# Splits of out-projection weights held behind softmax maxima, one FFN split moved back by one place, and the scaling of a head's output moved to the next head's second step

## The chip, the cores and the metric

The kernel runs on one core of a Trainium2 chip. The metric is the device time of one launch in microseconds (us). TensorE is PE in the profile (PEld is its weight load), VectorE is DVE, ScalarE is ACT, GpSimd is POOL, and SyncE, which only issues DMAs here, is SP. Every engine runs its own instructions strictly in the order in which they stand, and waits on semaphores for the others.

## The reference, cut to what matters

One transformer block on 512 tokens of width 1024 in fp32 (shapes after the batch and layer axes are dropped):

```python
h = rms_norm(x, attn_norm_g);  z = h @ w_in                    # 512 x 1952
y_mla  = softmax(q k^T * 96**-0.5 + mask) v                    # 8 heads, q and k 96 wide, v 64 wide
y_diff = rms_norm((softmax(q0 k0^T/8 + bias + mask)            # 4 heads, two maps of 64, v 128 wide
                 - lam * softmax(q1 k1^T/8 + bias + mask)) v, out_g) * (1 - lam_init)
x += concat[y_mla, y_diff] @ w_out                             # 1024 x 1024
g = rms_norm(x, ffn_norm_g) @ w_gate                           # 2816 wide
x += (silu(causal_dwconv3(g)) * (rms_norm(x, ffn_norm_g) @ w_up)) @ w_down
x += sigmoid(rms_norm(x, ple_norm_g) @ w_ple_gate) * (p @ w_ple_proj)
```

## The kernel before, in words

**Precision by splitting.** TensorE multiplies in a shortened fp32 format (fp32r). Each fp32 operand is therefore split into a rounded high part and a low remainder, and each product is made of three matmuls: high x high (L155), high x low (L156) and low x high (L157, in the helper `mm3`). `load_w` (L140 to L150) does this for a weight: one DMA on SP's queue brings 128x1024 floats (512 KB) into a buffer `raw` (L140), ACT casts it to `hi` (L148), DVE subtracts to get `lo` (L149). During attention there are three `raw` buffers, used in turn, so a DMA waits until the subtraction of the weight three places before it has read its buffer. The same pair of ACT cast and DVE subtraction makes the activations' halves: `split` (L183, L184; with a gain per channel L186, L187).

**Stages.** (1) From 0 to about 70 us, the norm and the projections. (2) From about 70 to 161 us, the loop over 32 slots (8 MLA heads x 4 blocks of 128 queries). Each slot makes the logits `ml` of the slot after it (PE), their negated maximum `nm` (DVE L570, L571), exp (ACT L573, tile `pm`), transposes `pm` on PE (L538, `pTm`), copies the result (`pt`; in odd steps ACT L541, in even steps DVE L543), and multiplies by V (PE L583, `mo`). Between these steps the projections for the second attention (`zd`) and later the first out-projection units are pumped as filling. (3) From about 161 to 224 us, the loop over 16 slots of the differential attention (`dslots`, 4 heads x 4 steps), which runs two slots ahead with the logits: PE makes two maps `dl`, one DVE instruction adds the bias strip and reduces to the maximum (L675, tiles `pmd`, `nmd`), ACT takes exp (L676), DVE joins both maps (L680 to L682), PE transposes (`pTd`), ACT copies (L541), PE multiplies by V (`do`). When a head's fourth step is through, `diff_pv` has ACT square and copy the output (`sqo`, `yd`, L696, L697), DVE reduce it (L699, L703), POOL take the power -1/2 (L704, `ro`), and DVE scale `yd` by `ro` (L706). Two steps into the next head `y_split` transposes it for the out-projection. The queries and keys of the next head come from `diff_T` (PE transposes `d0T` and `d1T`, split into the `st` tiles). Filling here is the out-projection (`wo_units`, tile `o`; DVE adds each finished block to `x`, L631). Its eight weights are `o00` to `o03` for the MLA half and `o10` to `o13` for the other half. (4) From about 224 to 250 us, the rest of the out-projection and the FFN's norm. (5) From about 250 to 600 us, the FFN: weights `wA`, `wT`, `wS` are split on ACT (L824) and DVE (L828), PE makes `g`, `gx`, `u` and so on from them, DVE does the convolution `cv` (L1112), and the down-projection `dn` follows. (6) The gate at the end.

**What sets the order.** PE's order is that of the program throughout (a manual schedule). For DVE and ACT a scheduler chooses the order in stage 2 (from its fifth slot on), 3 and 4; `tc.issue_after(ins)` tells it to place an instruction no earlier than behind `ins`. In the prologue and in the FFN's ramp (from L848 to the `region.__exit__` some 50 us into the FFN) DVE, ACT and POOL stand as written too. SP's DMAs stand in program order. In the loop before, the weights of `o` are loaded by `wo_w` when `wo_units` first asks for them, with nothing that holds their splits back; the scheduler has put the splits where its estimate found room, from 115 us on.

Of the kernel before, what the change touches and what calls it, by code (L numbers as in the profile page):

```python
# [15 lines left out]
ALU = mybir.AluOpType  # L16
# [4 lines left out]
P = 128  # L21
T = 512
NT = 4
# [4 lines left out]
H = 8  # L28
QK = 96
DH = 4  # L30
# [59 lines left out]
def _f32(ap):  # L90
    return ap.bitcast(F32)
# [3 lines left out]
def hybrid_block(ctx: ExitStack, tc: tile.TileContext, a: dict, out: bass.AP):  # L95
    nc = tc.nc
    V, S, G, TE = nc.vector, nc.scalar, nc.gpsimd, nc.tensor
# [11 lines left out]
    def bank(tag, name):  # L109
        return pp_.tile([P, 512], F32, tag=tag, bufs={"acc": 2, "lg": 3, "tp": 2, "ob": 1}[tag], name=name)  # L110

    def tt(name, dtype=F32):
        return att.tile([P, T], dtype, tag="tt", bufs=16, name=name)

    def sq_tile(name):
        return att.tile([P, D], F32, tag="sq", bufs=2, name=name)

    def pm_tile(name):
        return att.tile([P, T], F32, tag="pm", bufs=PM, name=name)
# [10 lines left out]
    def th_tile(name):  # L130
        return wts.tile([P, T], F32R, tag="th", bufs=8, name=name), wts.tile([P, T], F32R, tag="tl", bufs=8, name=name + "l")
# [6 lines left out]
    def load_raw(src, n, name):  # L138
        raw = wp["rawpool"].tile([P, 1024], F32, tag="raw", bufs=wp["raw"], name=f"raw_{name}")
        nc.sync.dma_start(raw[:, :n], src)  # L140
        return raw

    def load_w(src, n, name, eng=None):

        raw = load_raw(src, n, name)
        hi = wp["pool"].tile([P, 1024], F32R, tag="hi", bufs=wp["w"], name=f"hi_{name}")
        lo = wp["pool"].tile([P, 1024], F32R, tag="lo", bufs=wp["w"], name=f"lo_{name}")
        S.copy(hi[:, :n], raw[:, :n])  # L148
        (eng or V).tensor_tensor(lo[:, :n], raw[:, :n], _f32(hi[:, :n]), op=ALU.subtract)  # L149
        return hi, lo  # L150
# [153 lines left out]
    def d_hi(kq):  # L304
        raw = load_raw(a["w_d"][0, kq], 1024, f"d0{kq}")
        w = [wts.tile([P, 1024], F32R, tag=i, bufs=NW, name=f"{i}_d0{kq}") for i in ("hi", "lo")]
        zw.append(w)
        return (*hi(raw, w[0]), w[1])

    zw, zw1, zw2, wuq, wukv = [], [], [], [[], []], []  # L310
    d0 = d_hi(0)
# [168 lines left out]
    for t in range(NT):  # L480
        kv_ = kvb[:, t]
        sqk = sq_tile("sqk")[:, :H * 64].rearrange("p (h d) -> p h d", d=64)
        for c in range(2):
            hs = slice(4 * c, 4 * c + 4)
            ps = bank(UP_BANKS[(2 * t + c) % 4], f"ukv{t}{c}")
# [18 lines left out]
    for t in range(NT):  # L504
        q_ = xn_tile(f"qn{t}")[:, :H * QK].rearrange("p (h d) -> p h d", d=QK)
        sq = sq_tile("sqq")[:, :H * QK].rearrange("p (h d) -> p h d", d=QK)
        for c in range(2):
            hs = slice(4 * c, 4 * c + 4)
            ps = bank(UP_BANKS[(2 * t + c) % 4], f"uq{t}{c}")
# [50 lines left out]
    mla, ymn = {}, []  # L560
# [30 lines left out]
    strips = []  # L591
# [21 lines left out]
    def y_split(i, src, col, tag):  # L613

        ps = bank(tag, f"yT{i}")
        for t in range(NT):
            TE.transpose(ps[:, tsl[t]], src[:, tsl[t]], ident)
        yh[i], yl[i] = th_tile(f"yh{i}")
        split(yh[i], yl[i], ps, col)
# [10 lines left out]
    def add_x(b, ps):  # L630
        V.tensor_tensor(xb(b), xb(b), ps, op=ALU.add)  # L631

    wo2 = {}

    def wo_w(kq, dq):
        return load_w(a["w_out"][kq, dq], 1024, f"o{kq}{dq}")

    def wo_units(kq, dqs, nk):
# [13 lines left out]
    df = {}  # L652

    def diff_T(h, c):
        ps = bank("tp" if h else "acc", f"d{c}T{h}")
        for t in range(NT):
            TE.transpose(ps[:, tsl[t]], zd[c][t][:, h * P:(h + 1) * P], ident)
        h_, l_ = st[4 * (h % 2) + 2 * c], st[4 * (h % 2) + 2 * c + 1]
        split(h_, l_, ps, dcol if c == 0 else None)
        df["qk", h, c] = (h_, l_)  # L660

    def diff_logits(h, t):
        n = (t + 1) * P
        if t == 0:
            df["s0", h] = sm.tile([P, NT], F32, tag="s0", name="s0")
        s0 = df["s0", h][:, t:t + 1]
        (qh_, ql_), (kh_, kl_) = df["qk", h, 0], df["qk", h, 1]
        pms, s1 = [], sm.tile([P, 1], F32, tag="s1", bufs=4, name="s1")
        for m in range(2):
            r = slice(64 * m, 64 * m + 64)  # L670
            ps = bank("lg", f"dl{h}{t}{m}")
            mm3(ps[:, :n], [(qh_[r, tsl[t]], ql_[r, tsl[t]], kh_[r, :n], kl_[r, :n])])
            pm = pm_tile("pmd")
            nm = sm.tile([P, 1], F32, tag="nm", bufs=4, name="nmd")
            V.tensor_tensor_reduce(out=pm[:, :n], in0=ps[:, :n], in1=strips[0][:, h, T - n:], scale=1.0, scalar=3e38, op0=ALU.add, op1=ALU.min, accum_out=nm)  # L675
            S.activation(pm[:, :n], pm[:, :n], AF.Exp, bias=nm, scale=-1.0, accum_out=s0 if m == 0 else s1)  # L676
            pms.append(pm)

        cf = sm.tile([P, 1], F32, tag="cf", bufs=4, name="cf")
        V.reciprocal(cf, s1)  # L680
        V.scalar_tensor_tensor(cf, cf, nlam, s0, op0=ALU.mult, op1=ALU.mult)
        V.scalar_tensor_tensor(pms[0][:, :n], pms[1][:, :n], cf, pms[0][:, :n], op0=ALU.mult, op1=ALU.add)  # L682
        df["pm", h, t] = pms[0]

    def diff_pv(h, t):
        if t == 0:
            df["po"] = bank("ob", f"do{h}")
        po, pt = df["po"], df.pop(("pt", h, t))
        for j in range(t + 1):
            TE.matmul(po[:, tsl[t]], pt[:, tsl[j]], zd[2][j][:, h * P:(h + 1) * P], start=j == 0, stop=j == t)  # L690
        if t < NT - 1:
            return
        s0 = df["s0", h]
        yn = tt(f"yd{h}")
        sq = sq_tile("sqo")[:, :T]
        S.activation(sq, po, AF.Square)  # L696
        df["copy"] = S.copy(yn, po)  # L697
        sso = sm.tile([P, NT], F32, tag="sso", name="sso")
        V.reduce_sum(sso, sq.rearrange("p (t d) -> p t d", d=P), axis=AX.X)  # L699

        mo, ro = sm.tile([P, NT], F32, tag="mo", name="mo"), sm.tile([P, NT], F32, tag="ro", name="ro")
        V.scalar_tensor_tensor(mo, s0, EPS, s0, op0=ALU.mult, op1=ALU.mult)
        V.scalar_tensor_tensor(mo, sso, 1.0 / P, mo, op0=ALU.mult, op1=ALU.add)  # L703
        G.tensor_tensor(ro, mo, mhalf[:, :NT], op=ALU.pow)  # L704
        yv = yn.rearrange("p (t d) -> p t d", d=P)
        df["scale"] = V.tensor_tensor(yv, yv, ro.unsqueeze(2).broadcast_to([P, NT, P]), op=ALU.mult)  # L706
        df["y", h] = yn

    dslots = [(h, t) for h in range(DH) for t in range(NT)]
    x_sb = []  # L710
# [19 lines left out]
    for i, (h, t) in enumerate(slots):  # L730
        if i < 2:
            (mla_q, mla_k)[t](1)
        if i + 1 < len(slots):
            mla_logits(*slots[i + 1])
        if i == 4:
            region.__exit__(None, None, None)
            held = tc.issue_after(mla["nm"].ins)
            held.__enter__()
        if i == 8:
            held.__exit__(None, None, None)  # L740
            with tc.issue_after(mla["k"].ins):
                zd_norm(0)
        if 0 < h < H - 1 and t < 2:
            (mla_q, mla_k)[t](h + 1)
        if i == 1:
            lo(*z1_hi(3))
        if i in (9, 11, 13, 15):
            with tc.issue_after(mla["nm"].ins):
                zw2.append(load_w(a["w_d"][2, len(zw2)], 1024, f"d2{len(zw2)}"))
        if h < H - 1:  # L750
            pump(FILL_MLA[t])
        if i == 6:
            bias_strip()
        if h == H - 1:
            if t == 0:
                pump(100)
                fill.append(wo_units(0, range(4), 4))
            last_mla[t]()
        mla["pt", h, t] = probs_T(mla.pop(("pm", h, t)), t, f"m{h}{t}", t % 2)
        if i:  # L760
            mla_pv(*slots[i - 1])
# [3 lines left out]
    diff_T(1, 1)  # L765
    pump()
    y_split(3, ymn[3], None, "tp")
    for i, (h, t) in enumerate(dslots):
        if i + 2 < len(dslots):
            diff_logits(*dslots[i + 2])  # L770
        pump(FILL_DIFF[h][t])
        df["pt", h, t] = probs_T(df.pop(("pm", h, t)), t, f"d{h}{t}", True)
        if i:
            diff_pv(*dslots[i - 1])
        if h + 1 < DH and t == 0:
            diff_T(h + 1, 0)
        if t == 3 and h + 2 < DH:
            diff_T(h + 2, 1)
        if h and t == 2:
            y_split(4 + h - 1, df["y", h - 1], ocol, "tp")  # L780
        if h and t == 3:
            if h == 2:
                fill.append(wo_units(1, range(2), 2))
# [19 lines left out]
    for b in order[:6]:  # L803
        n = len(early)
# [22 lines left out]
    def lo_(h_, l_, src):  # L827
        V.tensor_tensor(l_, src, _f32(h_), op=ALU.subtract)  # L828
        return h_, l_
# [61 lines left out]
    for b in order:  # L891
        if b in early:
            ps = early[b]
            mm3(ps, wo_blocks(7, 8, b, wo2[b // 2]), False, True)
        else:
            ps = bank("tp" if b == 3 else "lg", f"o3{b}")
# [314 lines left out]
    d0 = down_hi(0)  # L1211
# [1 line left out]
    next(new)  # L1213
    next(g)
    up_split(2, cv2)
    dn0 = [lo_(*d0)]
    w5 = w_steps(5)
    old, g = g, new
    next(g)
    next(w5)  # L1220
    next(w4)
    next(old)
    w6 = w_steps(6)
# [6 lines left out]
    d0 = down_hi(1)  # L1230
# [80 lines left out]
    for b in (6, 7):  # L1311
        ps = bank("lg", f"dn4{b}")
# [27 lines left out]
    ps = [pg_bank(b) for b in range(4)]  # L1340
# [100 lines left out]
```

## Time and profile before

| | |
|---|---|
| median of 3 runs | 653.76 us (653.20, 653.76, 653.77) |
| the profiled execution | 653.42 us, its span in the profile 651.6 us |
| TensorE's granted clock | 1.000 |
| weights of `o`, first DMA issued, last cast begun | 103.4 us, 198.0 us |

The span begins with the first instruction in the trace and ends with the last; the other 1.8 us of the profiled execution lie outside it. All times in the trace count from the span's start. A row of the timeline gives start, duration, engine, line, operation, output, input, shapes, and in square brackets how long the engine had been idle before it and what it waited for. A row that was put together from x4 equal instructions has the time from the first one's start to the last one's end. On DVE and ACT an instruction begins 0.07 to 0.11 us before the one ahead of it ends, so a 1.22 us subtraction holds the next one back by 1.13 us.

### The profile page before, as it was taken

How to read it: one execution, taken by the hardware profiler on the slowest of the kernel's cores; microseconds unless marked ns; L12 is line 12 of the kernel's file. 1: busy time of each engine (PE TensorE's matmuls, PEld its weight loads, DVE VectorE, ACT ScalarE, POOL GpSimd, SP SyncE). 2: the span in 40 equal slices, each digit the busy share in tenths (PEclk: the TensorE clock that was granted, in tenths of full speed). 3: DMA queues.
4: the chain of work that ended last, by engine and by line, in shares of the span. 5: the costliest groups of instructions: out<-in, count | busy, mean ns of one | idle time of the engine just before them, and what ended most of it. 6: DMA issues, size and time to landing. Idle time of an engine off the chain costs nothing.

```text
span 651.6 us, 10276 instructions
## 1 busy us (share of the span) xinstructions
PE 641.6 (98%) x3932; PEld 569.5 (87%) x3932; DVE 475.2 (73%) x860; ACT 362.9 (56%) x631; POOL 56.6 (9%) x93
## 2 busy tenths in 40 slices
PE   9999999999999999999999999999999999999997
PEld 9988888888777778889999999999999999988886
DVE  6789587656878677888886767677767676759444
ACT  7797666457666455556554555455454545637211
POOL 1520040000000121000100000000010000000000
PEclk9999999999999999999999999999999999999999
DMA  8241235234100248636675646565646453531121
GB/s 303 96 162 40 91 73 171 66 115 144 33 33 2 64 179 254 162 70 178 174 215 127 179 114 181 122 197 116 179 114 177 116 176 114 179 130 60 38 80 49
DMA packets 29912, 82.63 MB, mean 127 GB/s; under 512 B 3100, under 2 KB 4124, under 8 KB 29736
## 3 DMA queue, kind: packets, MB, share of 16 engines
q1 hardware_dynamic: 23816, 69.17, 31.9%
q0 software_dynamic: 5616, 12.33, 11.1%
q8 instruction: 31, 0.51, 0.3%
q10 hardware_dynamic: 432, 0.49, 0.2%
q14 instruction: 17, 0.14, 0.1%
HBM read 77.77 MB, written 5.52 MB: 128 GB/s over the span
## 4 chain that ended last, share of the span: by engine, by line
PE 88%; DVE 7%; ACT 3%; issue 1%; DMA 1%; POOL 0%; ACTq 0%; DVEq 0%; POOLq 0%
PE dn L157 6%; PE dn L156 6%; PE dn L155 6%; PE gx L157 4%; PE gx L155 4%; PE gx L156 4%; PE g L155 4%; PE g L156 4%; PE g L157 4%; PE zd L155 3%; PE zd L157 3%; PE zd L156 3%; PE pg L155 2%; PE pg L157 2%; PE pg L156 2%; PE u L155 2%
## 5 line engine op out<-in xcount | busy, mean ns | idle before, releaser
L828 DVE TENSOR_TENSOR wSl<-rS,wSh 128x1024 fp32r<-128x1024 f32 x21 | 25.7, 1224 | 44.5 <-ACT wSh L824 44.4
L157 PE MATMUL dn<-ah,lo_dn 128*128 128x512 f32 x144 | 56.4, 392 | 0.0
L156 PE MATMUL dn<-al,hi_dn 128*128 128x512 f32 x144 | 56.3, 391 | 0.0
L155 PE MATMUL dn<-ah,hi_dn 128*128 128x512 f32 x144 | 56.0, 389 | 0.0
L945 POOL DMA_DIRECT2D rS<-in_w_gu x19 | 22.7, 1195 | 250.9 <-DVE cv L1112 115.0
L824 ACT CAST wSh<-rS 128x1024 fp32r<-128x1024 f32 x21 | 22.1, 1051 | 35.8 <-PE gy L156 35.5
L155 PE MATMUL zd<-hi_d,xh 128*128 128x512 f32 x96 | 39.4, 410 | 0.0
L156 PE MATMUL zd<-lo_d,xh 128*128 128x512 f32 x96 | 37.5, 391 | 0.0
L631 DVE TENSOR_TENSOR x<-x,dn 128x512 f32<-128x512 f32 x44 | 29.8, 678 | 6.5 <-PE dn L157 6.3
L828 DVE TENSOR_TENSOR wTl<-rA,wTh 128x1024 fp32r<-128x1024 f32 x19 | 23.3, 1224 | 14.9 <-ACT wTh L824 14.3
L573 ACT ACTIVATE pm<-ml,nm,rq 128x128 f32<-128x128 f32 (+3 forms) x32 | 19.7, 617 | 22.7 <-DVE nm L571 22.7
L157 PEld LDWEIGHTS dn<-ah,lo_dn 128*128 128x128 f32 x144 | 27.0, 187 | 5.7
L155 PEld LDWEIGHTS dn<-ah,hi_dn 128*128 128x128 f32 x144 | 27.1, 188 | 5.2
L156 PEld LDWEIGHTS dn<-al,hi_dn 128*128 128x128 f32 x144 | 27.0, 188 | 5.3
L155 PE MATMUL o<-yh,hi_o 128*128 128x512 f32 x64 | 26.9, 420 | 1.0 <-DVE x L631 1.0
L1115 ACT ACTIVATE cv<-cv 128x512 f32<-128x512 f32 x22 | 13.9, 631 | 24.5 <-DVE cv L1112 24.4
L824 ACT CAST wAh<-rA 128x1024 fp32r<-128x1024 f32 x21 | 22.0, 1050 | 9.1 <-DMA rA<-in_w_gu 9.1
L570 DVE TENSOR_REDUCE nm<-ml 128x1 f32<-128x128 f32 (+3 forms) x32 | 15.6, 486 | 15.3 <-PE ml L157 15.3
L155 PE MATMUL g<-b2h,wAh 128*128 128x256 f32 (+1 forms) x88 | 26.3, 299 | 0.1
L676 ACT ACTIVATE pmd<-pmd,nmd 128x128 f32<-128x128 f32 (+3 forms) x32 | 17.9, 560 | 15.1 <-DVE nmd L675 15.1
L156 PE MATMUL g<-b2l,wAh 128*128 128x256 f32 (+1 forms) x88 | 26.2, 297 | 0.0
L157 PE MATMUL g<-b2h,wAl 128*128 128x256 f32 (+1 forms) x88 | 26.2, 297 | 0.0
(467 smaller groups left out, 2226.8 us busy)
## 6 DMA issues: line engine op xcount, KB each, us to landing
rA<-in_w_gu SPq DMA_DIRECT2D x22, 512.0 KB, 3.9
rS<-in_w_gu SPq DMA_DIRECT2D x22, 512.0 KB, 3.5
rS<-in_w_gu POOLq DMA_DIRECT2D x19, 512.0 KB, 6.0
raw_dn<-in_w_down SPq DMA_DIRECT2D x18, 512.0 KB, 5.9
raw_d<-in_w_d SPq DMA_DIRECT2D x12, 512.0 KB, 3.7
r<-in_w_gu SPq DMA_DIRECT2D x19, 256.0 KB, 6.5
raw_o<-in_w_out SPq DMA_DIRECT2D x8, 512.0 KB, 3.7
rS_pg<-in_w_pg SPq DMA_DIRECT2D x6, 512.0 KB, 3.9
```

Of the source, the lines that this page charges most:

```text
L155: TE.matmul(ps, xh, wh, start=first and i == 0, stop=False, skip_group_check=again)
L156: TE.matmul(ps, xh, wl, start=False, stop=False, skip_group_check=again)
L157: TE.matmul(ps, xl, wh, start=False, stop=last and i == n - 1, skip_group_check=again)
L570: V.reduce_max(nm, ps[:, :n], axis=AX.X, negate=True)
L573: S.activation(pm[:, :n], ps[:, :n], AF.Exp, bias=nm, scale=r, accum_out=mla["ssum", h // 2][:, t, h % 2:h % 2 + 1])
L631: V.tensor_tensor(xb(b), xb(b), ps, op=ALU.add)
L676: S.activation(pm[:, :n], pm[:, :n], AF.Exp, bias=nm, scale=-1.0, accum_out=s0 if m == 0 else s1)
L824: S.copy(h_, src)
L828: V.tensor_tensor(l_, src, _f32(h_), op=ALU.subtract)
L945: nc.gpsimd.dma_start(sums[f].rearrange("p (i c) -> p i c", i=2), a["w_gu"][f][:, :2048].rearrange("p (i c) -> p i c", i=2)[:, :, :512], a ...
L1115: S.activation(cv, cv, AF.Silu)
```

## The change

Three edits, all in the order of the work; no arithmetic is changed.

1. The weights of `o` get a dictionary `wo_first`. Weight `o00` is now asked for in the third step of the last MLA head, and the scheduler is told to place its cast and its subtraction no earlier than behind the maximum of the last MLA slot (`mla["nm"]`). `o01`, `o02`, `o03`, `o10` and `o11` are asked for in the differential loop in slots 0, 3, 7, 10 and 12, each behind the maximum that was issued last (`df["nm"]`, which is that of two slots later). `wo_units` takes them from the dictionary. `o12` and `o13` are asked for after the loop as before.
2. `diff_pv` no longer issues the scaling `yd*ro` at once. It stores it, and the loop issues it in the second step of the next head. The last head is scaled at once, as before.
3. In the FFN's ramp the subtraction of the first down-projection weight (`lo_dn`) moves behind two generator steps, the second of which is that of `wAl` of unit 5.

```diff
+        if (kq, dq) in wo_first:
+            return wo_first.pop((kq, dq))
         return load_w(a["w_out"][kq, dq], 1024, f"o{kq}{dq}")
...
-            V.tensor_tensor_reduce(out=pm[:, :n], in0=ps[:, :n], in1=strips[0][:, h, T - n:], scale=1.0, scalar=3e38, op0=ALU.add, op1=ALU.min, accum_out=nm)
+            df["nm"] = V.tensor_tensor_reduce(out=pm[:, :n], in0=ps[:, :n], in1=strips[0][:, h, T - n:], scale=1.0, scalar=3e38, op0=ALU.add, op1=ALU.min, accum_out=nm)
...
-        df["scale"] = V.tensor_tensor(yv, yv, ro.unsqueeze(2).broadcast_to([P, NT, P]), op=ALU.mult)
         df["y", h] = yn
+        df["scaling"] = lambda: V.tensor_tensor(yv, yv, ro.unsqueeze(2).broadcast_to([P, NT, P]), op=ALU.mult)
+        if h == DH - 1:
+            df["scale"] = df["scaling"]()
...
+        if h == H - 1 and t == 2:
+            with tc.issue_after(mla["nm"].ins):
+                wo_first[0, 0] = wo_w(0, 0)
...
+    PRE = {0: (0, 1), 3: (0, 2), 7: (0, 3), 10: (1, 0), 12: (1, 1)}
...
+        if i in PRE:
+            with tc.issue_after(df["nm"].ins):
+                wo_first[PRE[i]] = wo_w(*PRE[i])
         if h + 1 < DH and t == 0:
             diff_T(h + 1, 0)
+        if h and t == 1:
+            df["scaling"]()
...
     up_split(2, cv2)
-    dn0 = [lo_(*d0)]
     w5 = w_steps(5)
     old, g = g, new
     next(g)
     next(w5)
+    dn0 = [lo_(*d0)]
     next(w4)
```

PE's 3592 rows of matrix work and POOL's rows stand in the same order before and after. On SP's queue five loads of `o` stood ahead of the four loads of `x`; now three do, and `o03` and `o10` stand behind them. Three places on DVE and ACT matter below.

The first is DVE at the end of the MLA loop, around the maxima of the last head's slots 2 and 3 (`ml72`, `ml73`); `yh0l` and `yh1l` are low halves of the attention's output, `pt` is the copy of the transposed probabilities of slot 2. Before:

```order
L570 TENSOR_REDUCE nm_1798<-ml72_1794 128x1
L149 TENSOR_TENSOR lo_o10_2532<-raw_o10_2529,hi_o10_2531 128x1024
L571 TENSOR_TENSOR nm_1798<-nm_1798,rq_502 128x1
L184 TENSOR_TENSOR st_117<-d1T0_1803,st_117 128x512
L570 TENSOR_REDUCE nm_1820<-ml73_1816 128x1
L184 TENSOR_TENSOR yh0l_1831<-yT0_1825,yh0_1830 128x512
L571 TENSOR_TENSOR nm_1820<-nm_1820,rq_502 128x1
L184 TENSOR_TENSOR yh1l_1840<-yT1_1834,yh1_1839 128x512
L543 COPY pt_1855<-pTm72_1851 128x384
```

DVE at the same place after:

```order
L570 TENSOR_REDUCE nm_1798<-ml72_1794 128x1
L571 TENSOR_TENSOR nm_1798<-nm_1798,rq_502 128x1
L184 TENSOR_TENSOR st_117<-d1T0_1803,st_117 128x512
L570 TENSOR_REDUCE nm_1820<-ml73_1816 128x1
L571 TENSOR_TENSOR nm_1820<-nm_1820,rq_502 128x1
L149 TENSOR_TENSOR lo_o00_1828<-raw_o00_1825,hi_o00_1827 128x1024
L184 TENSOR_TENSOR yh0l_1837<-yT0_1831,yh0_1836 128x512
L184 TENSOR_TENSOR yh1l_1846<-yT1_1840,yh1_1845 128x512
L543 COPY pt_1861<-pTm72_1857 128x384
```

The split between the two halves of the first maximum (of `o10`) is gone; instead that of `o00`, which stood at 115 us before, stands behind the second maximum and ahead of two low halves and the copy.

The second place is ACT in the differential loop, from head 0's last step to head 1's slot 1; `hi_o11` is the cast of weight `o11`, `pk` that of an input of the gate at the end. Before:

```order
L541 COPY pt_2115<-pTd03_2110 128x512
L797 CAST pk_2676<-raw_pT_2677 128x1024
L183 CAST st_117<-d1T2_2120 128x512
L676 ACTIVATE pmd_2132,s0_2039<-pmd_2132,nmd_2133 128x384
L676 ACTIVATE pmd_2140,s1_2127<-pmd_2140,nmd_2141 128x384
L541 COPY pt_2157<-pTd10_2155 128x128
L696 ACTIVATE sqo_2164<-do0_2037 128x512
L697 COPY yd0_2163<-do0_2037 128x512
L186 ACTIVATE st_117<-d0T2_2175,dcol_113 128x512
```

ACT at the same place after:

```order
L541 COPY pt_2115<-pTd03_2110 128x512
L183 CAST st_117<-d1T2_2126 128x512
L678 ACTIVATE pmd_2138,s0_2045<-pmd_2138,nmd_2139 128x384
L148 CAST hi_o11_2564<-raw_o11_2562 128x1024
L678 ACTIVATE pmd_2146,s1_2133<-pmd_2146,nmd_2147 128x384
L541 COPY pt_2163<-pTd10_2161 128x128
L698 ACTIVATE sqo_2170<-do0_2043 128x512
L699 COPY yd0_2169<-do0_2043 128x512
L186 ACTIVATE st_117<-d0T2_2180,dcol_113 128x512
```

The cast of `pk` has gone to the stage's end, and the cast of `o11` stands between the two exps of one slot. The casts of `o03` and `o13` stand likewise ahead of an exp: `hi_o03` of the loop's first one, `hi_o13` of the second one of slot (3,1).

The third place is DVE in the last differential head, from the first maximum of slot (3,3) on; in `mo` the power -1/2 is prepared, `yd2` is head 2's output, `x0` and `x1` are the residual stream. Before:

```order
L675 ISA pmd_2568,nmd_2569<-dl330_2564,strip_1098 128x512
L675 ISA nmd_2569 128x1
L703 SCALAR_TENSOR_TENSOR mo_2557<-sso_2555,mo_2557 128x4
L675 ISA pmd_2576,nmd_2577<-dl331_2572,strip_1098 128x512
L675 ISA nmd_2577 128x1
L706 TENSOR_TENSOR yd2_2551<-yd2_2551,ro_2558 128x512
L631 TENSOR_TENSOR x0_1843<-x0_1843,o11_2584 128x512
L680 RECIPROCAL cf_2580<-s1_2563 128x1
L702 SCALAR_TENSOR_TENSOR mo_2658<-s0_2424 128x4
L681 SCALAR_TENSOR_TENSOR cf_2580<-cf_2580,nlam_220,s0_2424 128x1
L682 SCALAR_TENSOR_TENSOR pmd_2568<-pmd_2576,cf_2580,pmd_2568 128x512
```

DVE behind the same maximum, after (the split of `o11` stands a few rows ahead of it):

```order
L684 SCALAR_TENSOR_TENSOR pmd_2519<-pmd_2527,cf_2531,pmd_2519 128x384
L677 ISA pmd_2581,nmd_2582<-dl331_2577,strip_1098 128x512
L677 ISA nmd_2582 128x1
L631 TENSOR_TENSOR x0_1849<-x0_1849,o11_2589 128x512
L709 TENSOR_TENSOR yd2_2551<-yd2_2551,ro_2558 128x512
L682 RECIPROCAL cf_2585<-s1_2568 128x1
L631 TENSOR_TENSOR x1_1851<-x1_1851,o12_2605 128x512
L683 SCALAR_TENSOR_TENSOR cf_2585<-cf_2585,nlam_220,s0_2424 128x1
L704 SCALAR_TENSOR_TENSOR mo_2658<-s0_2424 128x4
L149 TENSOR_TENSOR lo_o12_2667<-raw_o12_2664,hi_o12_2666 128x1024
L684 SCALAR_TENSOR_TENSOR pmd_2573<-pmd_2581,cf_2585,pmd_2573 128x512
```

The add to `x` now stands ahead of the scaling of `yd2`, the joining of the slot before (`pmd_2519`) comes later, and the split of `o12` has come in ahead of the last joining.

More of the change, by code (lines that the diff above doesn't have):

```diff
@@ L631, in add_x @@
         V.tensor_tensor(xb(b), xb(b), ps, op=ALU.add)
-    wo2 = {}
+    wo2, wo_first = {}, {}
     def wo_w(kq, dq):
+        if (kq, dq) in wo_first:
+            return wo_first.pop((kq, dq))
         return load_w(a["w_out"][kq, dq], 1024, f"o{kq}{dq}")
```

## The prediction

> **What bounds the kernel now.** I read the page first: the busy shares, then the chain that ended last.
>
> ```profile
> span 651.6 us, 10276 instructions
> PE 641.6 (98%) x3932; PEld 569.5 (87%) x3932; DVE 475.2 (73%) x860; ACT 362.9 (56%) x631; POOL 56.6 (9%) x93
> PE 88%; DVE 7%; ACT 3%; issue 1%; DMA 1%; POOL 0%; ACTq 0%; DVEq 0%; POOLq 0%
> ```
>
> TensorE has work in 98% of the span, and its order and work don't change. So the time can only change by what PE waits for DVE and ACT, 10 us in all, and only where the change moves rows. The view of the waits, for PE, lists them; these are the ones in the stages touched (us in all, times, longest):
>
> ```profile
> PE pTm L538 <- ACT pm L573: 1.1, 2, 0.9
> PE o L155 <- DVE x L631: 1.0, 1, 1.0
> PE gx L157 <- DVE wAl L828: 0.6, 1, 0.6
> PE kT L557 <- DVE st L187: 0.5, 2, 0.2
> PE dl L157 <- DVE st L187: 0.4, 1, 0.4
> ```
>
> That is 3.6 us, the most that better placed splits could win back by this view. Measured between the starts of PE's rows a stall is 0.1 to 0.2 longer than listed; I use starts. The view by tile of the moved weights gives the prices:
>
> ```profile
> L140 SPq DMA_DIRECT2D raw_o<-in_w_out x8: 327/328/341, 103.4 to 156.8; - x8
> L148 ACT CAST hi_o<-raw_o x8: 1030/1041/1053, 107.4 to 198.0; 128x1024 fp32r<-128x1024 f32 x8
> L149 DVE TENSOR_TENSOR lo_o<-raw_o,hi_o x8: 1212/1223/1226, 115.2 to 199.1; 128x1024 fp32r<-128x1024 f32 x8
> DMA to landing us min/median/max: 3.5/3.7/5.8
> ```
>
> A cast holds ACT for 1.04 us, a split DVE for 1.22 (1.13 from start to start), and a load lands 3.5 to 5.8 us after its issue. There are only three raw buffers. The load of `o03` waits for the split of `o00`, `o10` for `o01`, and so on. Holding a split behind a maximum therefore holds the load three places on, and ACT, which runs in order, stands at that load's cast until it lands. So the splits don't come "a step ahead": every one comes later than before, and the loads become tight. I take 3.65 us from issue to landing, just under the median of eight, since these loads are alone on the queue.
>
> **Part by part**, stage by stage, in time gained (−) or lost (+) on PE.
>
> *A, 119.9 us.* The split of `o00` leaves this place (it stood at 115.2).
>
> ```profile
> 116.31 2.49 DVE L401 TENSOR_TENSOR zd<-zd,rd 128x512 f32<-128x512 f32 x4
> 119.06 0.73 DVE L187 SCALAR_TENSOR_TENSOR st<-qT,qcol,st 96x512 fp32r<-96x512 f32 x1
> 119.85 0.64 PE L557 MATMUL kT<-ident,kvb 128*96 128x128 f32 x4 [0.25 <-DVE st L187]
> ```
>
> DVE's rows up to `st` move up by as much as 1.13, more than the stall of `kT` (0.4 between starts): **−0.45**.
>
> *B, 158 us.* The split of `o10` leaves, that of `o00` arrives.
>
> ```profile
> 155.52 1.21 DVE L149 TENSOR_TENSOR lo_o<-raw_o,hi_o 128x1024 fp32r<-128x1024 f32 x1
> 158.70 0.78 ACT L573 ACTIVATE pm<-ml,nm,rq 128x512 f32<-128x512 f32 x1
> 159.42 0.55 DVE L543 COPY pt<-pTm 128x384 f32<-128x384 f32 x1
> 160.12 0.79 PE L583 MATMUL mo<-kvb,pt 128*128 128x64 f32 x6
> ```
>
> The maximum no longer stands behind a split, so exp is early and the wait of `pTm` goes (−1.0). But between 155.5 and the copy at 159.42 one split leaves and one comes in. The copy stays where it was and ends at 159.97, while PE, now 1.0 earlier, wants it at 159.1. The `mo` that ran unhindered waits +1.0. The last slot's exp (158.70), behind two casts, costs an estimated +0.25. Together **+0.3** (bounds −1.0, if the copy isn't late, and +0.6).
>
> *C, 162 us.* The split of `o00` ends at 158.3; only then is `o03` issued. It lands at 162.0, and its cast stands ahead of the first exp of the differential loop:
>
> ```profile
> 161.85 0.40 ACT L676 ACTIVATE pmd<-pmd,nmd 128x128 f32<-128x128 f32 x1 [0.89 <-DVE nmd L675]
> ```
>
> That exp starts at 163.0 instead of 161.85. PE's filling with `o` covers most; left is **+0.2** (bounds 0 and 1.15).
>
> *D, 186 us.* The same with `o11`, between the two exps of slot (1,2).
>
> ```profile
> 174.98 1.23 DVE L149 TENSOR_TENSOR lo_o<-raw_o,hi_o 128x1024 fp32r<-128x1024 f32 x1
> 177.99 0.42 DVE L675 CUSTOM_DVE_ANT_0 pmd<-dl,strip 128x256 f32<-128x256 f32 x1
> 182.56 0.62 ACT L676 ACTIVATE pmd<-pmd,nmd 128x384 f32<-128x384 f32 x1 [0.69 <-DVE nmd L675]
> 184.27 0.71 ACT L186 ACTIVATE st<-d0T,dcol 128x512 fp32r<-128x512 f32 x1
> 185.57 0.74 DVE L187 SCALAR_TENSOR_TENSOR st<-d0T,dcol,st 128x512 fp32r<-128x512 f32 x1
> 186.41 0.28 PE L157 MATMUL dl<-st 64*128 64x128 f32 x1
> ```
>
> Without the split at 174.98 the maximum of slot (1,1) moves from 177.99 to about 177.1. The split of `o02` follows it and ends at 178.7; `o11` is issued then and lands at 182.4; its cast lasts to 183.4. The exp at 182.56 starts there, 0.85 later. Behind it on ACT are `sqo`, `yd` and the high half of `st`, then on DVE the low half, which ends at 187.2 rather than 186.3; the matmul at 186.41 waits for it: **+0.8** (0 for landings under 2.7 us, which let the cast end before 182.56; +3.0 at 5.8).
>
> *E, 203.8 us.* Here a split (1.13) and head 1's scaling stood ahead of `st`:
>
> ```profile
> 202.38 0.69 DVE L706 TENSOR_TENSOR yd<-yd,ro 128x512 f32<-128x512 f32 x1
> 202.99 0.74 DVE L187 SCALAR_TENSOR_TENSOR st<-d0T,dcol,st 128x512 fp32r<-128x512 f32 x1
> ```
>
> Both are gone from there, and with them `dl`'s stall: **−0.65** (bounds −0.4, the listed wait, and −0.8). The scaling itself moves some 4 us (a slot: 16 in 63 us) to the step before the transposes that read it, and costs nothing while it ends within that step.
>
> *F and G, 219 and 221.6 us.* The last head.
>
> ```profile
> 212.63 0.56 DVE L675 CUSTOM_DVE_ANT_0 pmd<-dl,strip 128x384 f32<-128x384 f32 x1
> 217.56 0.69 DVE L706 TENSOR_TENSOR yd<-yd,ro 128x512 f32<-128x512 f32 x1 [0.58 <-POOL ro L704]
> 218.17 0.68 DVE L631 TENSOR_TENSOR x<-x,o 128x512 f32<-128x512 f32 x1
> 219.22 0.75 DVE L682 SCALAR_TENSOR_TENSOR pmd<-pmd,cf 128x512 f32<-128x512 f32 x1
> 221.61 0.60 PE L538 MATMUL pTd<-ident,pmd 128*128 128x128 f32 x4
> ```
>
> The add to `x` for which `o` waited 1.0 no longer stands behind the scaling: −0.58 (its wait for POOL) and −0.61. But `o13` is issued when the split of `o10` ends (207.7), lands at 211.35, and its cast (to 212.4) stands ahead of the second exp of slot (3,1). The maximum at 212.63 comes at 213.95 (+1.3), and the split of `o11` stands behind it, ahead of the add (+1.13). Some 0.5 of the delay falls into DVE's waits in between. So the add ends 0.7 later, and **F is +0.7** (−1.0 if the cast is early and the split falls into a wait; +2.0). PE then reaches 221.61 about 0.9 late, at 222.5. The split of `o12` (221.0 to 222.2) now stands ahead of the joining of slot (3,3), which ends at 222.9 and is seen on PE 0.2 later: **G is +0.6** (0 to +1.1).
>
> *Gate weights.* Their loads (`raw_pT`, `raw_pp`) now stand behind those of `o` on SP; the last is issued at 222.2, and its split ends near 231. First use:
>
> ```profile
> 240.86 0.40 PE L155 MATMUL pp<-pk 128*128 128x512 f32 x1
> ```
>
> Ten us of cover: nothing.
>
> *H, the FFN's swap.*
>
> ```profile
> 301.35 1.04 ACT L824 CAST wAh<-rA 128x1024 fp32r<-128x1024 f32 x1
> 301.79 1.22 DVE L828 TENSOR_TENSOR lo_dn<-raw_dn,hi_dn 128x1024 fp32r<-128x1024 f32 x1
> 302.92 1.22 DVE L828 TENSOR_TENSOR wAl<-rA,wAh 128x1024 fp32r<-128x1024 f32 x1
> 304.06 1.22 DVE L828 TENSOR_TENSOR wSl<-rS,wSh 128x1024 fp32r<-128x1024 f32 x1
> 306.83 0.36 ACT L1068 COPY g<-gx 128x256 f32<-128x256 f32 x1 [1.75 <-DVE cv L1112]
> ```
>
> `wAl` can't start before its cast ends at 302.39. It gains 0.5 on 302.92, and `gx`'s wait goes (−0.6). But the 0.6 us from 301.79 to 302.4, which `lo_dn` filled, is now idle, so three splits that ended at 305.3 end at 305.9. `gx` with `wSl` waits +0.75, the convolution comes 0.65 later, and `g` behind the copy at 306.83 too: **+0.5** (bounds 0, if only the order within the three counts, and +0.75).
>
> *Sum:* −0.45 + 0.3 + 0.2 + 0.8 − 0.65 + 0.7 + 0.6 + 0.5 = **+2.0 us**. After 310 us PE runs without pause, so nothing takes it up. In C, D and F the landing time enters nearly one to one: 0.1 us on each load is about 0.3 in the sum, so 3.5 us gives +1.6 and 4.0 gives +3.1.
>
> [...]
>
> **The rivals.**
>
> *Hidden, within 0.2%* (1.3 us, about what a measurement of this kernel can tell from no change). The casts stand where the loads have landed: each load shorter than 3.4 us takes 0.75 or more off the sum, and at 2.7 us C, D and the late half of F vanish, which leaves about 0. For it: 3.5 is the shortest of eight loads, some of them beside others; in the new order all are alone. Against: none landed faster. Time 653.8 to 655.0. Chance 0.27. [...]
>
> *Faster.* The splits fall into DVE's idle time: it is 27% idle, 17 us of the 63 us loop, where eight splits need 9. Then the five listed waits go and nothing takes their place: 653.8 − 3.6 = 650.2. The place that decides is B: the copy of `pt` must end by 159.1 instead of 160.0, and the load of `o11` must land by 181.4. Against: the orders put one split on each side of that copy. Chance 0.11.
>
> *Much slower.* The held loads take 5.8 us, as the one beside the loads of `x` did. Then each of three casts costs 2.15 more: +8.5, 662. They stand alone, so 0.04.
>
> **The numbers.** The forecast, slower by more than 1.3, has 0.58. The profiled execution, 653.42 (span 651.6 and 1.8 around it), would become 655.4; it lies 0.3 under the median of the runs, so I give 653.76 + 2.0 = 655.8. The range takes in landings of 3.5 to 4.0 and the hidden case: 653.6 to 657.8. Slower is 0.58 + 0.04 = 0.62, same 0.27, faster 0.11.
>
> **What would show it.** Right: casts `hi_o` on ACT with waits for the DMA `raw_o` near 161, 182 and 211; no wait of `kT` near 120 and none of `pTm` near 158, with one of `mo` for DVE's copy in its place; `dl` near 187 waiting 0.8 for `st`, and none near 203; `lo_dn` behind `wAl`, and an idle DVE ahead of `wAl`. Wrong: casts that start without a wait, or a PE that loses nothing between 158 and 224.

## The result and the profile after

The changed kernel takes 659.15 us (median of five runs, 657.52 to 661.39), the kernel before 653.76; the ratio is 1.0069, 95% interval 1.0051 to 1.0088. That is slower, as forecast, but not by 2.0 us: by 4.5 (3.3 to 5.8) going by the ratio, by 5.4 between the medians. The median lies 1.35 us above the range's upper end of 657.8. The profiled execution took 657.52 us, 4.1 more than that of before. It is the only one of the five with a granted clock of 1.000; the other four have 0.991 to 0.996.

The page of the kernel after, its span and busy times:

```profile
span 655.7 us, 10264 instructions
PE 642.3 (98%) x3932; PEld 568.2 (87%) x3932; DVE 474.3 (72%) x860; ACT 364.0 (56%) x631; POOL 56.9 (9%) x93
```

PE has the same rows, and 0.7 us more busy time in a span that is 4.1 longer: the loss is waiting. The view of the waits for PE, after (us in all, times, longest):

```profile
PE o L155 <- DVE x L631: 1.3, 1, 1.3
PE do L692 <- ACT yd L699: 1.2, 1, 1.2
PE g L155 <- ACT g L1081: 0.8, 2, 0.4
PE mo L583 <- DVE pt L543: 0.8, 1, 0.8
PE dl L157 <- DVE st L187: 0.7, 1, 0.7
PE gx L157 <- DVE wSl L841: 0.6, 1, 0.6
PE pTm L538 <- ACT pm L573: 0.5, 2, 0.3
PE pTd L538 <- DVE pmd L684: 0.5, 1, 0.5
PE kT L557 <- DVE st L187: 0.2, 1, 0.2
```

Of the five waits that before had here, those of `dl` near 203 and of `gx` for `wAl` are gone, those of `kT` and `pTm` are down by 0.3 and 0.6, and that of `o` for `x` is up by 0.3. New are `mo` for DVE's copy, `dl` near 187, `gx` for `wSl`, one of the two of `g`, and `pTd`, all where the forecast had them, and two that it had not: `do` for ACT's copy of `yd`, and `g` near 292 (288 in before's time). The view by tile of the weights of `o`:

```profile
L148 ACT CAST hi_o<-raw_o x8: 1033/1047/1053, 107.8 to 212.7; 128x1024 fp32r<-128x1024 f32 x8
L149 DVE TENSOR_TENSOR lo_o<-raw_o,hi_o x8: 1207/1218/1220, 157.6 to 225.3; 128x1024 fp32r<-128x1024 f32 x8
DMA raw_o<-in_w_out: 4.6, 3
DMA to landing us min/median/max: 3.3/3.6/3.8
```

The first split has gone from 115.2 to 157.6 us and the last from 199.1 to 225.3. ACT stood idle 4.6 us in three places until a load had landed; before, 0.3 in one. The row on landings holds only six of the eight loads, before and after: those of `o03` and `o13` are not among them. From issue to cast these two took 3.6 and 4.4 us after. (The first row also corrects the description of the change: only the subtractions on DVE are held behind a maximum. The casts follow their loads, the first at 107.8.) The three places, from the timeline of ACT after, with what stands behind the last:

```profile
162.51 1.05 ACT L148 CAST hi_o<-raw_o 128x1024 fp32r<-128x1024 f32 x1 [2.08 <-DMA raw_o<-in_w_out]
182.87 1.05 ACT L148 CAST hi_o<-raw_o 128x1024 fp32r<-128x1024 f32 x1 [0.89 <-DMA raw_o<-in_w_out]
212.66 1.05 ACT L148 CAST hi_o<-raw_o 128x1024 fp32r<-128x1024 f32 x1 [1.67 <-DMA raw_o<-in_w_out]
213.62 0.51 ACT L678 ACTIVATE pmd<-pmd,nmd 128x256 f32<-128x256 f32 x1
215.99 0.61 ACT L678 ACTIVATE pmd<-pmd,nmd 128x384 f32<-128x384 f32 x1 [1.02 <-DVE nmd L677]
217.08 0.57 ACT L699 COPY yd<-do 128x512 f32<-128x512 f32 x1
```

And PE's timeline after, at the same place:

```profile
217.71 0.49 PE L692 MATMUL do<-zd,pt 128*128 128x128 f32 x2 [1.18 <-ACT yd L699]
220.89 0.50 PE L155 MATMUL o<-yh,hi_o 128*128 128x512 f32 x1 [1.29 <-DVE x L631]
```

Head 3's output `do` goes into the bank that head 2's output is still being copied from (the kernel has one bank for it, the tag `ob`). So PE waits for the copy (`yd`, 217.08), which stands behind the second exp of slot (3,2), which waits for DVE, which waits for the exp at 213.62, which stands behind the cast of `o13`.

Since PE's order is the same (3932 rows, as on the pages; the 3592 in the description of the change is a slip), each of its rows can be set against the same row of before. How much further back PE is behind each place than ahead of it, in us:

| place | forecast | profile after | e1, the same kernel again |
|---|---|---|---|
| A, `kT` 120 | −0.45 | −0.45 | −0.45 |
| B, 158 to 160 | +0.3 | +0.41 | +0.41 |
| C, 167 | +0.2 | −0.15 | −0.16 |
| D, `dl` 186 | +0.8 | +0.86 | +0.81 |
| E, `dl` 203 | −0.65 | −0.79 | −0.79 |
| F, `do` and `o`, 216 to 219 | +0.7 | +1.79 | +2.64 |
| G, `pTd` 221 | +0.6 | +0.67 | +0.51 |
| `g` 288 | none | +0.55 | +0.07 |
| H, 304 to 307 | +0.5 | +0.65 | +0.63 |
| from 119 us to the end | +2.0 | +3.47 | +3.33 |

The last row also holds small shifts between the places, of about 0.1 each. Another 0.6 and 0.34 lie ahead of 119 us, where no instruction was moved.

### The profile page after: what moved, and what is told of

Read it like the earlier page. It is cut to its first block, busy times and chain, and to the rows that moved or that the text cites. A ratio compares the mean times of both kernels' runs of the same rounds, so it can differ in the third digit from the quotient of the medians.

```text
span 655.7 us, 10264 instructions
## 1 busy us (share of the span) xinstructions
PE 642.3 (98%) x3932; PEld 568.2 (87%) x3932; DVE 474.3 (72%) x860; ACT 364.0 (56%) x631; POOL 56.9 (9%) x93
## 4 chain that ended last, share of the span: by engine, by line
PE 64%; DVE 6%; ACT 3%; DMA 1%; issue 1%; ACTq 0%; DVEq 0%
PE dn L157 6%; PE dn L156 6%; PE dn L155 6%; PE gx L157 4%; PE gx L155 4%; PE gx L156 4%; PE g L155 3%; PE g L156 3%; PE g L157 3%; PE pg L155 2%; PE pg L157 2%; PE pg L156 2%; PE o L155 2%; PE u L155 2%; PE u L157 2%; PE u L156 2%
## 5 line engine op out<-in xcount | busy, mean ns | idle before, releaser
L841 DVE TENSOR_TENSOR wAl<-rA,wAh 128x1024 fp32r<-128x1024 f32 x21 | 25.5, 1217 | 1.2 <-ACT wAh L837 1.2
```

## The experiments

All times are medians; ratios are against runs of the kernel before on the same chip, with the 95% interval. "From 119 us" is PE's shift in the profile, from just ahead of the first place that the change touches to the end, as in the table.

**e1: the changed kernel once more.**

> The changed kernel once more, unchanged. The profiled execution was 4.1 us longer than before, the median of the runs 5.4. Theory A (the loss is made of PE's waits, in the same places in every execution): again about +4 us, 657 to 658, with the granted clock of before's runs. Theory B (part of the loss is a lower granted clock, which some runs have): +5 us or more again, in runs whose clock is below 1.000, while runs at 1.000 lie near +4.

659.18 us (nine runs, 656.09 to 662.18) against 653.98; ratio 1.007 (1.0044 to 1.0096). The clock column of the runs tells more. Of nine runs five had a mean granted clock under 0.995; of some hundred runs of the kernel before in this study none had. The profiled execution of e1 (clock 0.997) shows the place. Its rows of `o` behind `do` start 0.43 us apart, where before they start 0.23 apart, and the table of busy times by stretches gives a granted clock of 0.56 from 218 to 220 us and 0.59 from 220 to 222 (the column ahead of the DMA share and the GB/s):

```profile
218.00:220.00 2.00, 1.90 (x6) 1.62 (x7) 2.00 (x9) 0.53 (x2) 0.98 (x1) 0.56 0.20 66
220.00:222.00 2.00, 2.00 (x6) 1.18 (x5) 2.00 (x7) 1.71 (x6) 0.03 (x1) 0.59 0.49 197
222.00:224.00 2.00, 2.00 (x15) 1.76 (x14) 2.00 (x5) 1.23 (x2) 0.00 (x0) 1.00 0.00 0
```

That stands behind a wait of `do` of 1.9 us. In the profile after, where `do` waited 1.18, the clock stayed at 1.0. So both theories have a part: the waits lie in the same places, and in most runs a lower clock comes on top.

**e2, e3, e4: one edit at a time,** each on the kernel before.

```diff
# e2: only the first edit
+            with tc.issue_after(df["nm"].ins):
+                wo_first[PRE[i]] = wo_w(*PRE[i])
# e3: only the second
+        if h and t == 1:
+            df["scaling"]()
# e4: only the third
     next(w5)
+    dn0 = [lo_(*d0)]
```

> Only the first edit: o's splits held behind the maxima, scaling and FFN as before. Theory A (held splits hold the three buffers, loads come late and ACT stands at their casts ahead of exps and of the head's output): most of the loss is here, +3 to +4 us, with casts of o03, o11 and o13 waiting for their loads near 161, 182 and 212, and PE waits for do, o and pTd between 215 and 222 that add up to 2 to 3 us. Rival (the scaling's new place or the FFN's swap carries the loss): under +1.5 us.

> Only the second edit: the scaling of a head's output in the second step of the next head. Theory A: the waits of dl near 203 (0.6) and of o near 219 (1.0) go, since the scaling no longer stands ahead of st and of the add to x, and nothing new comes: -1.7 us, faster than both kernels. Rival (the transposes of the next step wait for the later scaling): 0 to +1 us, with a wait of yT for DVE's yd.

> Only the third edit: lo_dn behind wAl in the FFN's ramp. By my sum +0.5 us (gx's wait for wAl of 0.6 goes, waits of gx for wSl and of g for ACT's copy of 0.7 and 0.6 come). Rival (the three splits cost the same in any order): 0, or -0.6 if only the wait that goes counts.

| | median | ratio | from 119 us |
|---|---|---|---|
| e2, held splits | 658.21 | 1.0067 (1.0045 to 1.009) | +4.61 |
| e3, scaling | 651.89 | 0.9968 (0.9954 to 0.9983) | −1.73 |
| e4, FFN swap | 655.10 | 1.0016 (1.0 to 1.0031) | +1.68, of it 0.65 at 304 to 307 and 0.57 at 288 |

The held splits carry the loss, and a little more than I had given them (+3 to +4; the medians differ by 4.2): F alone is +3.35 there. The long wait of PE in e2 and the one beside it:

```profile
PE do L692 <- ACT yd L699: 2.0, 1, 2.0
PE pTd L538 <- DVE pmd L684: 0.9, 2, 0.5
```

The load of `o13` took 5.4 us there from its issue to the cast (5.1 in e1, 4.4 in the profile after); those of `o03` and `o11` took 3.6 to 3.7 in all three. The scaling alone is 2.1 us faster than the kernel before: its list has neither a wait of `dl` near 203 nor of `o`, and none of `yT`. The swap loses +0.65 in its place, where +0.5 was forecast. The +0.57 at 288 isn't its doing: in five executions with the same rows around that place (the profile after and e1 to e4) that shift was 0.55, 0.07, 0.42, 0.18 and 0.57, in the same kernel once 0.55 and once 0.07. In the profile after, ACT waits 3.33 us near 257 for a store of the gate's inputs, 2.46 before, and its rows and DVE's are late from there on; that this makes the shift was not tried.

**e5, e6: the splits stay held, only casts move on ACT.** In e5 the cast of `o13` stands behind the last exp of slot (3,3) (and its split behind that slot's joining), in e6 those of `o03` and `o11` are moved back as well.

```diff
+    CAST = {(0, 3): (1, 0), (1, 1): (2, 0), (1, 3): (3, 3)}   # e5: the last only
-        S.copy(hi[:, :n], raw[:, :n])
+        with tc.issue_after(behind.ins) if behind else ExitStack():
+            S.copy(hi[:, :n], raw[:, :n])
```

> The changed kernel with one row of o moved on ACT: the cast of o13 stands behind the last exp of slot (3,3), not ahead of the second exp of slot (3,1), and its split behind that slot's joining. Theory A (ACT stands at that cast until a load lands that was held by the three buffers; the wait of do for ACT's copy, the slow rows behind it and the wait of o follow from this): no wait of do near 216 and none of o near 219, granted clock 1.0 there, pTd33 later waits some 1.7 for a cast of pk that comes ahead of the last exp; in all +1.4 us in the profile against before, a median near 655.5 and a narrower spread. Rival (the splits on DVE behind the maxima cost the time, whatever ACT does): as the changed kernel, 658 to 659.

> As e5, and the casts of o03 and o11 moved too, behind the exps of slots (1,0) and (2,0), where their loads have long landed. All of DVE's splits stay held behind their maxima. Theory A: the wait of dl for st near 187 (0.8) goes as well, +0.2 us against before, near 654.2. Rival (held splits): 658 or more.

e5: 655.42, ratio 1.0038 (1.0016 to 1.0059), from 119 us +1.14. e6: 655.81, ratio 1.0026 (1.001 to 1.0041), from 119 us −0.03. The waits of `do` and `o` are gone in both; F is −1.23 instead of +1.79, and in e6 D is −0.22 instead of +0.86. No cast of `o` waits for a load in e6. The narrower spread that was expected of e5 did not come: its runs lie from 654.06 to 660.98. What is left, from the waits of e6 and its timeline of ACT:

```profile
PE pTd L540 <- DVE pmd L689: 1.7, 1, 1.7
```

```profile
220.38 1.05 ACT L815 CAST pk<-raw_pT 128x1024 fp32r<-128x1024 f32 x1 [0.92 <-DMA raw_pT<-in_pT]
221.33 0.72 ACT L683 ACTIVATE pmd<-pmd,nmd 128x512 f32<-128x512 f32 x1
```

It is the same mechanism once more: now the cast of `pk` stands ahead of the last exp and waits for its load, which waited for a buffer. So the six splits held behind maxima cost little by themselves on DVE (`mo` still waits 0.8 for a copy that stands behind one); what costs is the cast on ACT ahead of an exp, waiting for a load that the three buffers held up. In runs at a clock of 0.998 or more e6 has 653.3 (two of twelve) and e5 654.4 (five); the others had less clock, and against my number the median of e6 is 1.6 us too long. In e6's profile, itself at 0.997, the low clock lies nowhere near the edits but at 23 to 27 us. One row of its waits, then the same stretch in before and in e6:

```profile
PE ssx L361 <- DVE xq L280: 0.2, 1, 0.2
24.00:26.00 2.00, 2.00 (x12) 1.98 (x11) 1.61 (x9) 1.58 (x3) 1.28 (x4) 1.00 0.16 40
24.00:26.00 2.00, 2.00 (x7) 1.90 (x7) 1.33 (x5) 1.52 (x4) 0.95 (x1) 0.50 0.51 167
```

There PE does nothing for some 2 us but 16 matmuls of one column each (`ssx`). Against before, PE falls back 1.6 us there. The profiles of e5, e7 and e12 have the same stretch. Five of the study's fourteen profiles list that wait of `ssx`, and four of these five have the stretch; of the nine that don't list it none has. Between 8 us and PE's last row every profile with a mean clock of 0.997 or less has a stretch at about half the clock (0.50 to 0.56 where it is lowest), here or behind `do` (that of e12, at 0.994, has both), and none at 0.998 or more has any. So a run's mean clock tells that there was such a stretch, not where; the kernel before has 0.997 or less in 29 of 106 runs. Why ten of e6's twelve runs have it stays open.

**e7, e8: a version that beats both, and the lost slot.** e7 is the scaling of e3 with one split held, that of `o10` behind the first maximum of the differential loop. e8 is the kernel before with `lo_dn` behind both weight splits and the convolution.

```diff
+    BEHIND = {(1, 0): ("nm", 0, 0)}          # e7, on e3
# e8, on the kernel before: behind next(w5), next(w4) and next(old)
     next(old)
+    dn0 = [lo_(*d0)]
```

> The kernel before with the second edit (scaling) and with one held split: that of o10 behind the first maximum of the differential loop, so that it no longer stands between the two halves of the maximum of MLA slot (7,2). By the rows: the wait of pTm near 158 goes (-1.0, of which 0.25 comes back at the next pTm and some 0.2 at 167), the rest as with the scaling alone: -2.2 us in the profile, near 651.4. Rival (mo then waits for DVE's copy as in the changed kernel): as the scaling alone, 651.9.

> The kernel before with lo_dn moved further back than in the third edit, behind both weight splits and the convolution. If the third edit loses because an idle place of DVE (301.8 to 302.4) is given up and everything behind is 0.65 late, then here gx's wait for wAl (0.6) goes, none of wSl or g comes near 306, and the split is paid near 312 to 316 instead: 0 us in all. If the order of wAl and lo_dn alone mattered, -0.5 us.

e7: 652.27, ratio 0.9973 (0.996 to 0.9987), from 119 us −1.97, of which +0.53 at 288. The wait of `pTm` goes as worked out (B is −0.54), but the runs don't tell it from e3: it is faster than before, and whether by more than the scaling alone stays unclear. e8: 654.04, ratio 0.9996 (0.998 to 1.0011), −0.01 from 119 us. DVE's timeline of e8:

```profile
302.67 1.23 DVE L828 TENSOR_TENSOR wAl<-rA,wAh 128x1024 fp32r<-128x1024 f32 x1 [0.55 <-ACT wAh L824]
303.81 1.22 DVE L828 TENSOR_TENSOR wSl<-rS,wSh 128x1024 fp32r<-128x1024 f32 x1
306.40 1.21 DVE L828 TENSOR_TENSOR lo_dn<-raw_dn,hi_dn 128x1024 fp32r<-128x1024 f32 x1
```

The 0.55 us ahead of `wAl` is the idle place that `lo_dn` filled before. H gains 0.5 there and it is paid back by 316 us: the swap loses what DVE leaves empty.

**e9 to e12: a wait of PE without any load.** On e3, added copies on ACT into a scratch tile that nothing reads delay head 2's square and copy, and with them `do`. No weight, split or load moves.

```diff
+        if h == 2:
+            with tc.issue_after(df["exp32"].ins):
+                for _ in range(6):          # e9: 4, e12: 7; e11: five wider ones and one of 440
+                    last = S.copy(scr[0], strips[0][:, 0, :256])
```

> The kernel with the scaling alone (second edit), and four added copies of 128x256 on ACT into a scratch tile that nothing reads, placed behind the last exp of slot (3,2) and ahead of head 2's square and copy. No load and no split moves. They delay the copy of yd2 by some 1.8 us, of which 1.2 were spare: do waits 0.5 to 0.8 us for it. Both theories of the clock: no loss of clock after so short a wait; +0.7 us on the scaling alone's 651.9, 652.6.

> The same with six added copies; the last falls behind the first exp of slot (3,3), so that the copy of yd2 comes 3 us or more later and do waits about 2 us. Theory C (a wait of PE of 1.9 us or more before do is enough to halve the granted clock for some 3 us, whatever made PE wait): the rows behind do run at half speed, mean clock 0.997 or less in nearly all runs, and the loss on the scaling alone is the wait and 0.5 to 1.5 us more: +2 to +3, near 654.5. Rival (the slow rows in the changed kernel came from the load or the held weights, not from the wait): rows behind do at full speed, clock as with the scaling alone, +1.3, 653.2.

> As e10, with wider added copies (five of 128x288, one of 128x440), so that do waits about 2.0 us instead of 1.75, as long as in the runs of the changed kernel and of the held splits alone in which the rows behind do ran at half speed. If the length of this one wait decides: the rows behind run at half speed, the clock is 0.997 or less in nearly all runs, near 655. If it doesn't (another wait beside it, or something else, belongs to it): full speed, 653.57 + 0.25 = 653.8.

> Seven added copies of 128x256, of which the last comes behind the second exp of slot (3,3): do waits about 3.0 us. If long waits lower the clock at all: rows behind do at half speed for some 3 us, clock near 0.997, +1.2 for the wait and 0.5 to 1.5 for the clock on e10's 653.57, 655.5 to 656.5. If they don't: 654.8 with a clock of 0.999.

| | wait of `do` | median | ratio | runs with a clock of 0.996 or less |
|---|---|---|---|---|
| e3, none added | 0 | 651.89 | 0.9968 (0.9954 to 0.9983) | 0 of 12 |
| e9 | 0.3 | 652.05 | 0.9969 (0.9954 to 0.9985) | 2 of 11 |
| e10 | 1.7 | 653.57 | 0.9986 (0.9972 to 1.0001) | 0 of 12 |
| e11 | 2.0 | 655.55 | 1.0018 (1.0 to 1.0036) | 9 of 12 |
| e12 | 2.7 | 656.17 | 1.0033 (1.0015 to 1.005) | 9 of 12 |

e10 did less than theory C wanted, e11 what it wants: 0.3 us more of waiting cost 2.0 us. The runs of e10 and e11 come from two chips; the kernel before had 0.996 or less in 4 of 22 runs on the one and in 3 of 23 on the other, so the chip doesn't explain 0 of 12 against 9 of 12. PE's timeline in e10, then in e11 (start, duration):

```profile
217.11 0.49 PE L693 MATMUL do<-zd,pt 128*128 128x128 f32 x2 [1.75 <-ACT yd L705]
217.35 0.47 PE L155 MATMUL o<-yh,hi_o 128*128 128x512 f32 x1
217.66 0.39 PE L156 MATMUL o<-yh4l,hi_o 128*128 128x512 f32 x1
217.89 0.39 PE L157 MATMUL o<-yh,lo_o 128*128 128x512 f32 x1
218.12 0.40 PE L155 MATMUL o<-yh,hi_o 128*128 128x512 f32 x1
```

```profile
216.97 0.49 PE L693 MATMUL do<-zd,pt 128*128 128x128 f32 x2 [2.04 <-ACT yd L706]
217.22 0.48 PE L155 MATMUL o<-yh,hi_o 128*128 128x512 f32 x1
217.53 0.59 PE L156 MATMUL o<-yh4l,hi_o 128*128 128x512 f32 x1
217.92 0.63 PE L157 MATMUL o<-yh,lo_o 128*128 128x512 f32 x1
218.34 0.63 PE L155 MATMUL o<-yh,hi_o 128*128 128x512 f32 x1
...
220.48 0.63 PE L157 MATMUL o<-yh,lo_o 128*128 128x512 f32 x1
220.91 0.43 PE L155 MATMUL o<-yh,hi_o 128*128 128x512 f32 x1
```

The rows start 0.43 apart instead of 0.23, from about 0.6 us behind the wait's end until 220.9. The stretches of e11 give the clock:

```profile
214.00:217.00 3.00, 0.96 (x7) 0.55 (x5) 2.22 (x7) 2.97 (x8) 0.00 (x0) 1.00 0.00 0
218.00:221.00 3.00, 3.00 (x9) 2.32 (x8) 2.34 (x5) 0.00 (x0) 0.52 (x1) 0.50 0.00 0
221.00:224.00 3.00, 3.00 (x25) 2.75 (x23) 0.92 (x2) 1.44 (x3) 0.00 (x0) 1.00 0.27 70
```

In e11's own runs, the three with a clock of 0.998 or more have a median of 653.9 and the six at 0.996 one of 655.6: such a stretch cost an estimated 1.7 us, the difference of the two medians. Which of the nine had theirs behind `do` and which only behind `ssx` is known for the profiled one alone: behind `do`. The profile of e12 has it there too. In e11's trace the slow rows run from 217.53 to 220.91 us, at a granted clock of 0.50 from 218 to 221. Going by the clock of the runs, the wait of 2.0 us left 0.996 or less in 9 of 12, and the one of 1.75 us in none. How long a wait has to be, and what else has to come with it, these runs don't show.

## Why the prediction was right and wrong

**Right.** The direction, its chance of 0.62, and the mechanism: held splits hold the three buffers, the loads come late, and ACT stands at their casts. A, B, D, E, G and H came within 0.15 us of their terms. C was +0.2 and came out as −0.15: the first exp was late as worked out (163.46, with its cast at 162.51), and PE's filling covered all of it.

**Wrong, first: the term F.** It was +0.7, "an add that ends 0.7 later", and measured +1.79 in the profile after, +2.64 in e1 and +3.35 in e2. Two things in that step failed. The load of `o13` was priced at 3.65 us from issue to landing, and took 4.4, 5.1 and 5.4 to its cast (the median and the range that the price was taken from were of six loads, not eight). And I followed the delay on DVE to the add to `x` only. Its other end is ACT: the copy of `yd` came at 217.08 instead of 214.38, and `do`, which before had started 1.2 us after that copy had ended, used that slack up and waited first. The bound of +2.0 that I gave for F held in the profile after and not in the others. e5 shows the cause: with this one cast and its split elsewhere F is −1.23. The profile of before had a warning on the price: its one cast that waited for its load, `o00`, began 4.05 us after the issue at 103.39.

**Wrong, second: the clock.** The sum had no term for it, since the granted clock of before was 1.000. The longer waits of PE for `do` had slow rows behind them: in the profiles of e1, e2, e11 and e12 (waits of 1.9, 2.0, 2.0 and 2.7 us) those ran at about half the clock (0.56, 0.51, 0.50 and 0.51 in the lowest stretch), and the medians of e11 and e12 lie 3.7 and 4.3 us above that of e3. That this happens without any late load was shown in e11 and e12; that it happens in the changed kernel is seen in e1's and e2's profiles, at the same rows. In the runs of e1 with a clock of 0.998 or more the kernel takes 656.8 (two runs), 3.0 over before's runs with such a clock (653.7); the medians of all differ by 5.2. So some 2 us of the loss in the medians go with the clock. The range was made from waits alone; its upper end of 657.8 lay 0.9 above the sum for landings of 4.0 us (653.76 + 3.1 = 656.9), for which no reason was given, and was still too low.

**The rivals.** "Hidden" falls: no load that ACT had to wait for in the profile after took less than 3.58 us to its cast (3.58 for `o03`, 3.67 for `o11`, 4.42 for `o13`), where the case wanted 3.4 or less. "Faster" counted 17 us of idle DVE in the loop, by the mean over the whole kernel; the loop itself had 12.4 (50.6 us busy of 63). It fell where it was said to be decided: DVE's copy of `pt` ended at 160.53 and `mo` waited 0.8 for it. "Much slower" had a price of 5.8 us for each load, and one of the three came near it, `o13` in e2 with 5.4.

**Not in the sum:** 0.6 us ahead of 119 us and 0.55 at 288 us in the profile after. They vary between executions of one kernel, and no edit touches them. Their cause was not tried.

## What to carry to other kernels

Holding a subtraction behind something critical also holds the buffer that it reads; look up how many buffers there are, find the load that waits for this one, and see what stands behind that load's cast on its engine (here the exp at 213.62 behind the cast of `o13`, which had waited 1.67 us). Follow a delay to every engine that the delayed row feeds, and take the one with the least slack, not the one that waited before. Of three edits that came together, one was worth 2.1 us and was hidden by the other two: time them apart. And look at the clock of every run, not only at that of the profiled one.

## What the runs showed of the hardware

- In e11's profile TensorE's wait of 2.0 us for `do` was followed by 3.4 us of rows 0.43 apart instead of 0.23 (217.53 to 220.91), at a granted clock of 0.50; 9 of its 12 runs have a clock of 0.996 or less, and none of e10's, with a wait of 1.75 us. By the medians of e11 and e3 (655.55 and 651.89) that stall cost an estimated 3.7 us. A stretch of some 2 us with 16 one-column matmuls (`ssx`) and a wait of 0.2 ahead of them was followed by a clock of 0.50 or 0.51 from 24 to 26 us in four of five profiles (e5, e6, e7 and e12; 1.00 in the profile after); what decides there was not tried.
- In the profiles of the kernel after, e1 and e2 a load of 512 KB with no other load beside it took 3.6 to 3.7 us from issue to cast for `o03` and `o11`, and 4.4, 5.1 and 5.4 for `o13`. In the view of the DMA for 207 to 214 us these three have a tail at 23 GB/s, and one packet of an instruction queue (q8) that takes 1.2%, 1.9% and 2.1% of 16 engines' seven microseconds, 1.3, 2.1 and 2.4 us; the windows of the fast loads have no such packet. The kernel before has it in this window too (0.8%, 0.9 us), with no load beside it. That this packet holds up the load's last packets is argued from that alone; it wasn't tried.
